# Layer 1 of a two-layer trunk: low weight parts from DRAM, an even/odd convolution on VectorE, and a 6:2 split of the channel tiles

## The chip, the cores and the metric

The kernel runs on one core of a Trainium2 chip. The metric is the device time of one execution in microseconds. A run's own time is a little longer than the span of its profile, which goes from the first to the last instruction. The engines are TensorE (PE; its weight loads PEld), VectorE (DVE), ScalarE (ACT), GpSimd (POOL) and SyncE (SP), which issues every DMA of this kernel, in program order.

## What is computed

A decoder trunk of two layers over 2048 positions of 1024 channels, each `x + RMSNorm_post(mixer(RMSNorm_pre(x)))`. Layer 0 is windowed attention beside a pooling mixer. Layer 1, which the change touches:

```python
def odd_mixer(h, w_in, dw_w, dw_b, ln_g, ln_b, w_out):
    proj = h @ w_in
    a, b, gate = jnp.split(proj, [CONV_WIDTH, 2 * CONV_WIDTH], axis=-1)
    glu = a * jax.nn.sigmoid(b)
    conv = lax.conv_general_dilated(
        glu, dw_w.astype(glu.dtype), window_strides=(1,), padding=[(CONV_K - 1, 0)],
        dimension_numbers=('NWC', 'WIO', 'NWC'), feature_group_count=CONV_WIDTH)
    cf = conv.astype(jnp.float32) + dw_b.astype(jnp.float32)
    mu = jnp.mean(cf, axis=-1, keepdims=True)
    var = jnp.mean(jnp.square(cf - mu), axis=-1, keepdims=True)
    cn = (cf - mu) * lax.rsqrt(var + EPS) * ln_g.astype(jnp.float32) + ln_b.astype(jnp.float32)
    y = jax.nn.silu(cn).astype(h.dtype) * jax.nn.silu(gate)
    return y @ w_out
```

## The kernel before

**Tiles and stages.** Channels lie on the 128 partitions, so 1024 channels are 8 tiles (k or i, 0 to 7). The 2048 positions are done in two halves of 1024, each in two blocks of 512 columns. Layer 0 runs for both halves, then layer 1: `inproj1` with `gates1` for half 0 and for half 1 (24 weight tiles of `wc` per half: for each channel tile the one of the tanh gate and the one of the value, then eight of the output gate), and then `outproj` with `wo1`, whose eight weight tiles are taken for each of four half and block pairs: 32 uses, called w0 to w31 here. w16 is the first of half 1, w24 the first of the last block.

**Products.** `project` makes a 512-column block of one weight tile with 24 matmuls: for each of 8 k, weights rounded to fp32r (`wh`) with the rounded part of the data (`hi`), `wh` with the rest of the data (`lo`), and the rest of the weights (`wl`) with `hi`. `w_load` brings raw weight tiles (512 KB) into three `wr` slots; `w_split` copies them to `wh` on ScalarE and forms `wl` as raw minus `wh` on VectorE. There are two slots each of `wh` and `wl`.

**Convolution.** For five of the eight channel tiles `conv_dve` runs 31 taps over 1024 columns per half on VectorE, two of them plain multiplies and 29 multiply-adds, in two alternating sums, and adds these. For three tiles (2, 4, 6) `conv_pe` does the taps of both halves as 16 groups of three 128x128 matmuls on TensorE with weights built on the host (`toep`). The results go through DRAM: `cd` (VectorE tiles), `ct` (TensorE tiles); the gates go through `sg`, a tile of two k for each half and block.

**Norm.** `norms` loads the eight results of a half, sums them, and for each block takes mean and variance (`norm_block`); `apply` then does for each k: times the reciprocal root, Silu, times the gate, and the split into `hi` and `lo`, the mix tile that `outproj` multiplies. Post-norm and residual of a finished block follow on VectorE while the next block is on TensorE.

**Order.** Nothing is written out by hand. `Flow` is a planner that runs while the program is built: the main line emits TensorE work, side tasks (generators with a priority) are stepped when their inputs are ready by the planner's own costs, and the order in which they emit is the order on each engine. `get` and `put` take and return slots of the SBUF pools (`s4` has 37 slots of 4 KB per partition), `until` waits for a condition. Each operation is recorded at one line, that of the helper (L189 before, L190 after), so the rows name tiles: `mm` products, `a` convolution or mean sums in PSUM, `s` a tile of the s4 pool, `packed` small constants.

Of the kernel before, what the change touches and what calls it, by code (L numbers as in the profile page):

```python
# [27 lines left out]
HIST = CK - 1  # L28
NJ = (CK + PH - 1 + PH - 1) // PH
# [5 lines left out]
DVE_CONV = (0, 1, 3, 5, 7)  # L35
# [9 lines left out]
    ("sinks", 8), ("post", 2 * KT), ("icnt", 64), ("tri", 2 * P), ("pscale", 4), ("dwn", len(DVE_CONV) * CK), ("dwb", KT), ("dwbp", KT * GPT),  # L45
# [162 lines left out]
def trunk_kernel(tc, a):  # L208
# [395 lines left out]
    gc = const([P, len(DVE_CONV), HIST], "gc")  # L604

    def constants():
# [7 lines left out]
        V.tensor_scalar(dwb, dwb, 2.0, None, op0=ALU.mult)  # L614
        V.tensor_scalar(dwbp, dwbp, 2.0, None, op0=ALU.mult)
# [410 lines left out]

    def conv_dve(half, i, slot, gl, over):
        acc = []
        for _ in range(2):
            acc.append((yield from get("s4")))  # L1030
        V.tensor_scalar(acc[0], gl[:, 0:TH], dwn[:, slot, 0:1], dwb[:, i:i + 1], op0=ALU.mult, op1=ALU.add)
        yield flow.t["P"]
        V.tensor_scalar(acc[1], gl[:, 1:1 + TH], dwn[:, slot, 1:2], None, op0=ALU.mult)
        for k in range(2, CK):
            yield flow.t["P"]
            r = acc[k % 2]
            V.scalar_tensor_tensor(r, gl[:, k:k + TH], dwn[:, slot, k:k + 1], r, op0=ALU.mult, op1=ALU.add)
# [54 lines left out]
    def glu(bank, at, ths, b, gv, n):  # L1092
# [42 lines left out]
    def apply(half, k, b, cfs, rbs, sgs, mix, done, left):  # L1135
# [4 lines left out]
        if key not in sgs:  # L1140
            yield from until(lambda: (half, *key) in stored)
# [4 lines left out]
        yield V.tensor_tensor(out=c, in0=c, in1=halves(g)[k % 2], op=ALU.mult)  # L1146
        t = yield from get("s4", TH, F32R)
# [10 lines left out]
    def norms(half, over, mix, done):  # L1158
        yield from until(lambda: len(over[half]) >= 5 and (half == 0 or len(dones[half - 1]) >= KT))
        cfs, rbs, sgs, left, loaded = {}, {}, {}, {}, []  # L1160

        def load():
            for n in range(KT):
                yield from until(lambda: len(over[half]) > n)
# [12 lines left out]
        for n in range(1, KT):  # L1177
# [168 lines left out]
```

## Time and profile before

| | before |
|---|---|
| median of 3 runs | 1501.53 us (1500.33 to 1501.77) |
| the profiled execution's own time | 1503.71 us |
| span of its profile | 1500.8 us |
| mean granted TensorE clock, share of full | 0.991 |
| TensorE busy | 1469.3 us (98%) |
| VectorE busy | 1250.2 us (83%) |
| ScalarE busy | 565.2 us (38%) |
| DMA | 186.46 MB, mean 124 GB/s |

In its profile, layer 1 begins at about 697 us, the out-projection of layer 1 at 1282 us, its half 1 at 1379 us, its last block at 1441 us. A line of --lines form reads: line, engine, operation, output<-inputs, shapes, count, then busy us and mean ns of one, then the engine's idle time just before and what ended it. Matmuls overlap in the records, so their mean exceeds their share of the time.

### The profile page before, as it was taken

How to read it: one execution, taken by the hardware profiler on the slowest of the kernel's cores; microseconds unless marked ns; L12 is line 12 of the kernel's file. 1: busy time of each engine (PE TensorE's matmuls, PEld its weight loads, DVE VectorE, ACT ScalarE, POOL GpSimd, SP SyncE). 2: the span in 40 equal slices, each digit the busy share in tenths (PEclk: the TensorE clock that was granted, in tenths of full speed). 3: DMA queues.
4: the chain of work that ended last, by engine and by line, in shares of the span. 5: the costliest groups of instructions: out<-in, count | busy, mean ns of one | idle time of the engine just before them, and what ended most of it. 6: DMA issues, size and time to landing. Idle time of an engine off the chain costs nothing.

```text
span 1500.8 us, 19112 instructions
## 1 busy us (share of the span) xinstructions
PE 1469.3 (98%) x7226; PEld 1193.0 (79%) x7226; DVE 1250.2 (83%) x1927; ACT 565.2 (38%) x1069; POOL 49.1 (3%) x65
## 2 busy tenths in 40 slices
PE   8999999999999999999999999999999999998997
PEld 6877778788877778788888888888888888776796
DVE  7888775777887766577899999999999999989885
ACT  6454432454444423454211123211212134666551
POOL 0000000000000000000100000000000000000000
PEclk9999999999999999999999999999999999999898
DMA  6112312455411101355421224422544744836574
GB/s 221 57 54 80 97 44 59 140 175 176 145 33 33 46 29 56 99 178 187 166 63 55 82 85 136 172 71 67 182 148 137 236 144 137 256 127 229 165 251 154
DMA packets 107468, 186.46 MB, mean 124 GB/s; under 512 B 32240, under 2 KB 56432, under 8 KB 107376
## 3 DMA queue, kind: packets, MB, share of 16 engines
q1 hardware_dynamic: 107376, 185.25, 39.3%
q8 instruction: 56, 0.92, 0.3%
q14 instruction: 36, 0.29, 0.1%
HBM read 146.42 MB, written 38.80 MB: 123 GB/s over the span
## 4 chain that ended last, share of the span: by engine, by line
PE 92%; DVE 3%; DMA 2%; ACT 1%; issue 1%; SPq 0%; POOL 0%; POOLq 0%; DVEq 0%; ACTq 0%
PE mm L189 81%; PE a L189 5%; PE pv L189 3%; PE pt L189 2%; DVE s L189 2%; DMA s<-in_toep 1%; DVE t L189 1%; DVE wl L189 0%; DMA s<-in_xn 0%; DMA gt<-s 0%; ACT s L189 0%; DMA s<-sg 0%; SPq L189 0%; ACT wh L189 0%; ACT t L189 0%
## 5 line engine op out<-in xcount | busy, mean ns | idle before, releaser
L189 PE MATMUL mm<-s,wh 128*128 128x512 f32 (+1 forms) x3616 | 1139.6, 396 | 13.3 <-ACT s L189 7.4
L189 PEld LDWEIGHTS mm<-s,wh 128*128 128x128 f32 x3616 | 669.5, 189 | 164.6 <-DVE s L189 10.7
L189 PE MATMUL mm<-s,wl 128*128 128x512 f32 (+1 forms) x1808 | 709.9, 393 | 0.0
L189 PEld LDWEIGHTS mm<-s,wl 128*128 128x128 f32 x1808 | 341.4, 189 | 76.2
L189 DVE SCALAR_TENSOR_TENSOR s<-s,packed,s 128x1024 f32<-128x1024 f32 x290 | 354.6, 1279 | 0.0
L189 ACT ACTIVATE wh<-wr 128x1024 fp32r<-128x1024 f32 (+1 forms) x138 | 145.4, 1054 | 368.8 <-PE mm L189 315.9
L189 DVE TENSOR_TENSOR wl<-wr,wh 128x1024 fp32r<-128x1024 f32 (+1 forms) x138 | 167.7, 1215 | 74.9 <-ACT wh L189 72.8
L189 ACT ACTIVATE t<-mm 128x512 f32<-128x512 f32 (+1 forms) x122 | 68.5, 562 | 98.6 <-PE mm L189 90.3
L189 DVE TENSOR_TENSOR t<-t,t 128x512 f32<-128x512 f32 (+1 forms) x131 | 86.2, 663 | 17.3 <-ACT t L189 15.4
L189 ACT ACTIVATE s<-mm 128x512 f32<-128x512 f32 (+1 forms) x116 | 67.9, 585 | 78.2 <-PE mm L189 70.8
L189 PE MATMUL a<-s,s 128*128 128x128 f32 (+2 forms) x592 | 90.5, 290 | 1.1 <-DMA s<-in_toep 0.9
L189 PEld LDWEIGHTS a<-s,s 128*128 128x128 f32 x592 | 81.1, 190 | 11.1 <-DMA s<-in_toep 2.8
L189 DVE TENSOR_TENSOR s<-s,s 128x512 f32<-128x512 f32 (+3 forms) x100 | 85.0, 874 | 3.3 <-DMA s<-ct 1.0
L189 ACT ACTIVATE s<-t 128x512 fp32r<-128x512 f32 (+1 forms) x52 | 48.8, 938 | 64.4 <-DVE t L189 64.1
L189 DVE TENSOR_TENSOR s<-t,s 128x512 fp32r<-128x512 f32 (+1 forms) x56 | 52.4, 935 | 22.1 <-ACT s L189 20.9
L189 ACT ACTIVATE t<-s 128x512 f32<-128x512 f32 x80 | 48.8, 628 | 50.7 <-DVE s L189 42.4
L189 DVE TENSOR_TENSOR t<-pt,packed 128x512 f32<-128x512 f32 x64 | 44.1, 690 | 28.4 <-PE pt L189 27.9
L189 ACT ACTIVATE s<-s,st 128x128 f32<-128x128 f32 x128 | 49.6, 389 | 25.0 <-DVE st L189 24.9
L189 POOL TENSOR_TENSOR rs<-ms,mhalf 128x4 f32<-128x4 f32 (+1 forms) x21 | 24.9, 1186 | 791.8 <-DVE ms L189 787.7
L189 DVE SCALAR_TENSOR_TENSOR s<-t,mm 128x512 f32<-128x512 f32 x48 | 40.1, 836 | 8.1 <-PE mm L189 6.2
L189 ACT ACTIVATE s<-xh 128x512 fp32r<-128x512 f32 x48 | 29.9, 630 | 39.9 <-DVE xh L189 39.5
L189 PEld LDWEIGHTS pv<-t,s 128*64 128x64 f32 x480 | 25.1, 136 | 23.2 <-issue 7.2
(100 smaller groups left out, 928.3 us busy)
## 6 DMA issues: line engine op xcount, KB each, us to landing
wr<-in_wo SPq DMA_DIRECT2D x64, 512.0 KB, 3.7
wr<-in_wc SPq DMA_DIRECT2D x48, 512.0 KB, 3.7
wr<-in_wa SPq DMA_DIRECT2D x27, 512.0 KB, 3.7
s<-in_toep SPq DMA_DIRECT2D x24, 384.0 KB, 4.3
xr<-in_xp SPq DMA_DIRECT2D x32, 256.0 KB, 4.1
x<-s SPq DMA_DIRECT2D x32, 256.0 KB, 3.2
xh<-x SPq DMA_DIRECT2D x32, 256.0 KB, 3.6
sg<-s SPq DMA_DIRECT2D x16, 512.0 KB, 4.8
```

What stands on the lines that cost most here:

```text
L189: fn(*args, **kw)
```

## The change

- `w_lows`, a task of low priority that starts at 60 us, forms the low parts of the 32 distinct layer 1 weight tiles once, during layer 0 (load, copy on ScalarE, subtract on VectorE, store to DRAM `wcl` and `wo1l`). `w_split` then loads `wl` by DMA in layer 1 and leaves out the subtract.
- `conv_dve` splits the positions by parity. `both` is even plus odd; three chains of half length run over even, odd and `both` (16, 15 and 16 taps, the last with sums of neighbouring taps), and even and odd outputs come from their sums and differences.
- Six channel tiles go to VectorE (0, 1, 3, 4, 6, 7), two to TensorE (2, 5).
- `norms` of half 1 starts when the program has emitted the last gate weight (`gated`), no longer when half 0's mix tiles are done; `apply` takes a gate load or a mix tile only if more than three s4 slots are free or `gated` holds; loads of results follow the additions (`added`); norm tasks of half 1 have a priority lower by one.

The diff, cut:

```diff
-DVE_CONV = (0, 1, 3, 5, 7)
+DVE_CONV = (0, 1, 3, 4, 6, 7)
...
+    def w_lows():
+        yield 60.0
+        for name, i in lows:
+            yield from until(lambda: avail["s4"] > 5)
+            raw = (yield from get("s4")).rearrange("p (k f) -> p k f", k=KT)
+            wl = (yield from get("s4", TH, F32R)).rearrange("p (k f) -> p k f", k=KT)
+            yield Q.dma_start(out=raw, in_=a[name][i])
+            yield A.activation(wl, raw, AF.Copy)
+            at = V.tensor_tensor(out=wl, in0=raw, in1=wl.bitcast(F32), op=ALU.subtract)
+            put(raw)
+            yield at
+            Q.dma_start(out=kept[name, i], in_=wl.bitcast(F32))
+            put(wl)
+            formed.add((name, i))
...
+                if (name, i) in kept:
+                    yield from until(lambda: (name, i) in formed)
+                    Q.dma_start(out=wl.bitcast(F32), in_=kept[name, i])
                 yield A.activation(wh[:, ks], raw[:, ks], AF.Copy)
-                V.tensor_tensor(out=wl[:, ks], in0=raw[:, ks], in1=wh[:, ks].bitcast(F32), op=ALU.subtract)
+                if (name, i) not in kept:
+                    V.tensor_tensor(out=wl[:, ks], in0=raw[:, ks], in1=wh[:, ks].bitcast(F32), op=ALU.subtract)
...
+        V.tensor_tensor(out=both, in0=even, in1=odd, op=ALU.add)
+        for m in range(HJ + 1):
+            for r, x, w, bias in ((ya, even, dwn[:, slot, HIST - 2 * m:CK - 2 * m], dwb), (yb, odd, dwn[:, slot, HIST - 1 - 2 * m:HIST - 2 * m] if m < HJ else None, None), (yc, both, dws[:, slot, HJ - m:HJ + 1 - m], dwb2)):
+                if w is None:
+                    continue
+                yield flow.t["P"]
+                xs = x[:, HJ - 1 - m:HJ + n - m] if x is odd else x[:, HJ - m:HJ + n - m]
+                if m:
+                    V.scalar_tensor_tensor(r, xs, w, r, op0=ALU.mult, op1=ALU.add)
...
+        V.tensor_tensor(out=cv[:, 0], in0=ya.rearrange("f (s q) -> f s q", s=SG), in1=yb[:, :n].rearrange("f (s q) -> f s q", s=SG), op=ALU.add)
+        V.tensor_tensor(out=ya, in0=ya, in1=yb[:, 1:], op=ALU.add)
+        yield flow.t["P"]
+        at = V.tensor_tensor(out=cv[:, 1], in0=yc.rearrange("f (s q) -> f s q", s=SG), in1=ya.rearrange("f (s q) -> f s q", s=SG), op=ALU.subtract)
...
         if key not in sgs:
-            yield from until(lambda: (half, *key) in stored)
+            yield from until(lambda: (half, *key) in stored and (avail["s4"] > 3 or gated))
             g = yield from get("s4")
             sgs[key] = (g, Q.dma_start(out=g, in_=sg_t[(half, *key)]))
...
+        yield from until(lambda: avail["s4"] > 3 or gated)
         t = yield from get("s4", TH, F32R)
...
-        yield from until(lambda: len(over[half]) >= 5 and (half == 0 or len(dones[half - 1]) >= KT))
+        yield from until(lambda: len(over[half]) >= 5 and (half == 0 or gated))
...
-                yield from until(lambda: len(over[half]) > n)
+                yield from until(lambda: len(over[half]) > n and added[0] >= n - 2)
...
-            flow.spawn(block(b), 1 + b)
+            flow.spawn(block(b), 1 + b + half)
...
         gates1(half, now)
+    gated.append(1)
```

**How the order moves, first place: SP where the out-projection begins.** `wr` is a raw weight tile, `wl` (from `wo1l`) a low part, `s<-sg` a gate tile, `s<-cd` and `s<-ct` results of the convolution, `sg<-s` a store; the waits in brackets are for lanes of the DMA queue or for engines. Before, from the raw tile of w3 on (the next one is that of w4):

```order
L189 DMA wr_10021<-in_wo 128x1024 [waits DMAHW6_49,DVE_49]
L189 DMA sg_3_0_102<-s_1549_9909 128x1024 [waits DMAHW7_49,Activation_49]
L189 DMA s_1576_10078<-sg_3_0_94 128x1024 [waits DMAHW0_49,PE_49]
L189 DMA s_1580_10107<-sg_0_1_89 128x1024 [waits DMAHW1_49,PE_49]
L189 DMA wr_10114<-in_wo 128x1024 [waits DMAHW2_49,DVE_49]
L189 DMA sg_3_1_103<-s_1559_9963 128x1024 [waits DMAHW3_49,Activation_49]
L189 DMA s_1585_10143<-cd_1_79 128x1024 [waits DMAHW4_49,PE_49]
L189 DMA s_1586_10145<-ct_75 128x16x64 [waits DMAHW5_49,PE_49]
L189 DMA s_1587_10147<-cd_1_81 128x1024 [waits DMAHW6_49,PE_49]
```

With the change, from the row behind the raw tile of w4 to the low part of w2:

```order
L190 DMA s_1633_10546<-sg_3_0_94 128x1024 [waits DMAHW6_49,DMAHW5_49,DVE_49]
L190 DMA s_1634_10548<-sg_3_0_94 128x1024 [waits DMAHW7_49]
L190 DMA s_1635_10550<-cd_1_77 128x1024
L190 DMA s_1636_10552<-ct_74 128x16x64 [waits DMAHW0_49]
L190 DMA s_1637_10554<-cd_1_79 128x1024 [waits DMAHW1_49]
L190 DMA s_1638_10556<-sg_0_1_89 128x1024 [waits DMAHW2_49]
L190 DMA s_1639_10558<-sg_0_1_89 128x1024 [waits DMAHW3_49]
L190 DMA s_1640_10560<-sg_1_1_91 128x1024 [waits DMAHW4_49]
L190 DMA sg_3_1_103<-s_1619_10414 128x1024 [waits DMAHW5_49,Activation_49]
L190 DMA s_1643_10602<-cd_1_81 128x1024 [waits DMAHW6_49]
L190 DMA s_1644_10604<-ct_75 128x16x64 [waits DMAHW7_49]
L190 DMA wl_10612<-wo1l_134 128x1024 [waits DMAHW0_49,PE_49]
```

Before, two gate tiles stood ahead of the raw tile of w4 and the loads of half 1 behind it, each with a wait for TensorE; now eleven transfers, most without such a wait, stand between the raw tile of w4 and the low part of w2, whose slot comes free with the last matmul of w0. Two gate tiles are loaded twice.

**Second place: SP where half 1 of the out-projection begins.** Before, the last two gate tiles of half 1's first block (2 and 3):

```order
L189 DMA wr_10918<-in_wo 128x1024 [waits DVE_49]
L189 DMA s_1735_10932<-sg_2_0_100 128x1024 [waits DMAHW4_49,PE_49]
L189 DMA out_y<-s_1624_10343 128x512 [waits DMAHW5_49,DVE_49]
L189 DMA out_y<-s_1624_10343 128x512 [waits DMAHW6_49,DVE_49]
L189 DMA xr_10938<-x_0_0_104 128x512 [waits DMAHW7_49,DMAHW1_49]
L189 DMA xr_10942<-x_0_0_104 128x512 [waits DMAHW2_49,DMAHW0_49]
L189 DMA s_1739_10949<-sg_3_0_102 128x1024 [waits PE_49]
```

With the change, the low part of w17 and a raw tile, then the same two gate tiles:

```order
L190 DMA wl_11403<-wo1l_133 128x1024 [waits DMAHW6_49,PE_49]
L190 DMA wr_11412<-in_wo 128x1024 [waits DMAHW7_49,Activation_49]
L190 DMA s_1803_11439<-sg_2_0_100 128x1024 [waits DMAHW0_49]
L190 DMA s_1808_11462<-sg_3_0_102 128x1024 [waits DMAHW1_49]
L190 DMA s_1809_11465<-sg_0_1_97 128x1024 [waits DMAHW2_49]
```

The gate tiles now come behind a low part that waits for the last matmul of w15.

**Third place: DVE, up to the last mix tile of w16's block.** Before, from the multiply by the last gate tile to the subtract that forms the last `lo`:

```order
L189 TENSOR_TENSOR s_1591_10155<-s_1591_10155,s_1739_10949 128x512 [waits DMAHW1_49]
L189 TENSOR_TENSOR s_1627_10363<-s_1627_10363,t_1702_10746 128x512
L189 TENSOR_SCALAR ms_10986<-pt_10978 128x4 [waits PE_49]
L189 CAST rh_10991<-rs_10989 128x4 [waits Pool_49]
L189 TENSOR_TENSOR s_1749_10993<-s_1591_10155,s_1749_10993 128x512 [waits Activation_49]
L189 TENSOR_TENSOR s_1627_10363<-s_1627_10363,s_1739_10949 128x512 [waits Activation_49]
L189 TENSOR_TENSOR rh_10991<-rs_10989,rh_10991 128x4 [waits DVE_49]
L189 CAST rh_11004<-rs_10999 128x4 [waits Pool_49]
L189 TENSOR_TENSOR s_1753_11008<-identr,rh_10991 128x512
L189 TENSOR_TENSOR s_1753_11008<-identr,rh_10991 128x512 [waits DVE_49]
L189 TENSOR_TENSOR rh_11004<-rs_10999,rh_11004 128x4 [waits DVE_49]
L189 TENSOR_TENSOR s_1752_11006<-s_1627_10363,s_1752_11006 128x512 [waits Activation_49]
```

With the change, the last twelve rows of such a piece, which begins 14 rows higher with the multiply that waits for gate tile 2; `x2` is a row for two instructions, 28 in all, one of them on four columns:

```order
L190 TENSOR_TENSOR s_1816_11497<-s_1659_10672,s_1816_11497 128x512 [waits Activation_49]
L190 TENSOR_TENSOR s_1691_10878<-s_1691_10878,t_1775_11297 128x512
L190 TENSOR_TENSOR s_1817_11504<-s_1635_10550,s_1817_11504 128x512 [waits Activation_49]
L190 TENSOR_TENSOR s_1637_10554<-s_1637_10554,s_1809_11465 128x512
L190 TENSOR_TENSOR s_1636_10552<-s_1636_10552,t_1792_11391 128x512
L190 TENSOR_TENSOR s_1738_11114<-s_1738_11114,xr_11491 128x512 [waits DMAHW7_49,DVE_49]
L190 TENSOR_TENSOR s_1691_10878<-s_1691_10878,s_1808_11462 128x512 [waits Activation_49]
L190 TENSOR_TENSOR s_1738_11114<-s_1738_11114,xr_11494 128x512 [waits DMAHW0_49,DVE_49]
L190 TENSOR_TENSOR s_1818_11514<-s_1637_10554,s_1818_11514 128x512 [waits Activation_49]
L190 TENSOR_TENSOR s_1643_10602<-s_1643_10602,t_1792_11391 128x512
L190 SCALAR_TENSOR_TENSOR s_1761_11231<-s_1761_11231,packed,t_1811_11475 128x512 x2
L190 TENSOR_TENSOR s_1819_11517<-s_1691_10878,s_1819_11517 128x512 [waits Activation_49]
```

Before, from the first multiply with gate tile 2 to that last subtract there were 21 instructions, six of them on tiles of four columns (`ms`, `rh`); now post-norm and residual of half 0's second block (`packed`, `xr`) stand among them.

## Rows read from the trace of the kernel before

**Rows 1.** The page, busy time and 40 slices.
```profile
PE 1469.3 (98%) x7226; PEld 1193.0 (79%) x7226; DVE 1250.2 (83%) x1927; ACT 565.2 (38%) x1069; POOL 49.1 (3%) x65
...
PE   8999999999999999999999999999999999998997
...
DVE  7888775777887766577899999999999999989885
```

**Rows 2.** Windows: us; PE, PEld, DVE, ACT, POOL busy; granted clock, DMA share, GB/s.
```profile
697.00:1282.00 585.00, 583.97 (x2695) 480.56 (x2694) 547.57 (x547) 141.53 (x230) 22.23 (x26) 1.00 0.41 128
60.00:543.00 483.00, 479.43 (x2610) 378.33 (x2609) 372.26 (x897) 211.35 (x511) 13.42 (x16) 1.00 0.29 88
1282.00:1441.00 159.00, 150.17 (x633) 119.48 (x632) 142.81 (x211) 92.98 (x142) 5.16 (x4) 0.95 0.62 199
1050.00:1100.00 50.00, 49.20 (x261) 41.20 (x260) 46.76 (x43) 9.31 (x22) 1.06 (x4) 1.00 0.50 154
1385.00:1390.00 5.00, 3.06 (x10) 2.41 (x11) 4.04 (x9) 2.00 (x4) 1.44 (x1) 0.55 0.83 319
1440.00:1450.00 10.00, 10.00 (x87) 10.00 (x86) 8.40 (x14) 6.83 (x12) 1.01 (x1) 1.00 1.00 327
```

**Rows 3.** The chain that ended last: start us, us, step; three like these two.
```profile
1060.22 2.94 PE a L189 x24
...
1174.08 2.68 PE a L189 x24
```

**Rows 4.** Groups of instructions by form, whole span.
```profile
L189 DVE SCALAR_TENSOR_TENSOR s<-s,packed,s 128x1024 f32<-128x1024 f32 x290 | 354.6, 1279 | 0.0
L189 DVE SCALAR_TENSOR_TENSOR s<-s,packed,t 128x512 f32<-128x512 f32 x56 | 40.1, 746 | 4.0 <-ACT t L189 4.0
L189 ACT ACTIVATE wh<-wr 128x1024 fp32r<-128x1024 f32 (+1 forms) x138 | 145.4, 1054 | 368.8 <-PE mm L189 315.9
L189 DVE TENSOR_TENSOR wl<-wr,wh 128x1024 fp32r<-128x1024 f32 (+1 forms) x138 | 167.7, 1215 | 74.9 <-ACT wh L189 72.8
```

**Rows 5.** ScalarE in order of time: start us, us, copies of w1, w2, w3.
```profile
1282.33 1.06 ACT L189 ACTIVATE wh<-wr 128x1024 fp32r<-128x1024 f32 x1 [0.64 <-PE mm L189]
...
1289.01 1.06 ACT L189 ACTIVATE wh<-wr 128x1024 fp32r<-128x1024 f32 x1 [0.57 <-ACT s L189]
...
1294.56 1.06 ACT L189 ACTIVATE wh<-wr 128x1024 fp32r<-128x1024 f32 x1 [1.78 <-PE mm L189]
```

**Rows 6.** SP in order of time: start us, us, issue.
```profile
1284.68 0.33 SPq L189 DMA_DIRECT2D wr<-in_wo  x1
...
1296.20 3.85 SPq L189 DMA_DIRECT2D s<-sg  x1
...
1380.66 0.38 SPq L189 DMA_DIRECT2D s<-sg  x1
```

**Rows 7.** DMA issues, us to landing: whole span twice, then at 1284.68, 1296.20, 1380.66, 1400:1450.
```profile
wr<-in_wo SPq DMA_DIRECT2D x64, 512.0 KB, 3.7
s<-sg SPq DMA_DIRECT2D x16, 512.0 KB, 5.4
wr<-in_wo SPq DMA_DIRECT2D x1, 512.0 KB, 4.3
s<-sg SPq DMA_DIRECT2D x1, 512.0 KB, 7.7
s<-sg SPq DMA_DIRECT2D x1, 512.0 KB, 5.3
s<-x SPq DMA_DIRECT2D x2, 512.0 KB, 7.2
```

**Rows 8.** TensorE in order of time: the start of w16, its last k.
```profile
1379.48 0.49 PE L189 MATMUL mm<-s,wh 128*128 128x512 f32 x1
...
1397.27 0.80 PE L189 MATMUL mm<-s,wh 128*128 128x512 f32 x1 [0.88 <-DVE s L189]
```

**Rows 9.** VectorE in order of time, from the multiply with gate tile 2.
```profile
1386.07 1.29 DVE L189 TENSOR_TENSOR s<-s,s 128x512 f32<-128x512 f32 x2 [0.93 <-DMA s<-sg]
...
1396.53 0.68 DVE L189 TENSOR_TENSOR s<-s,s 128x512 fp32r<-128x512 f32 x1
```

More of the change, by code (lines that the diff above doesn't have):

```diff
@@ L322, in trunk_kernel @@
     wraw, wready, last = [], [], set()
+    lows = [x for n, x in enumerate(wseq) if x[0] in ("wc", "wo1") and x not in wseq[:n]]
+    kept = {(name, i): dr.tile([P, KT, P], F32, tag=f"{name}l_{i}", name=f"{name}l_{i}") for name, i in lows}
+    formed = set()
+    def w_lows():
[12 more added lines that the diff above has]
+            formed.add((name, i))
     def w_load(go):
@@ L614, in constants @@
         V.tensor_scalar(dwb, dwb, 2.0, None, op0=ALU.mult)
+        V.tensor_scalar(dwb2, dwb, 2.0, None, op0=ALU.mult)
+        pairs_of = dwn[:, :, 1:].rearrange("p i (m r) -> p i m r", r=2)
+        V.tensor_tensor(out=dws[:, :, 1:], in0=pairs_of[:, :, :, 0], in1=pairs_of[:, :, :, 1], op=ALU.add)
+        V.tensor_copy(dws[:, :, :1], dwn[:, :, :1])
         V.tensor_scalar(dwbp, dwbp, 2.0, None, op0=ALU.mult)
@@ L1025, in last_block, with parities @@
             put(*w)
+    def parities(gl):
+        return gl.rearrange("f (r j) -> f r j", r=2)
     def conv_dve(half, i, slot, gl, over):
[L1028 to L1037, printed above, removed]
+        n = TH // 2
+        even, odd = parities(gl)[:, 0, :], parities(gl)[:, 1, :]
+        ta = yield from get("s4", 2 * n + HJ)
+        tb = yield from get("s4", 2 * n + 1)
+        both, ya = ta[:, :n + HJ], ta[:, n + HJ:]
+        yb, yc = tb[:, :n + 1], tb[:, n + 1:]
+        V.tensor_tensor(out=both, in0=even, in1=odd, op=ALU.add)
[7 more added lines that the diff above has]
+                    V.scalar_tensor_tensor(r, xs, w, r, op0=ALU.mult, op1=ALU.add)
+                elif bias is None:
+                    V.tensor_scalar(r, xs, w, None, op0=ALU.mult)
+                else:
+                    V.tensor_scalar(r, xs, w, bias[:, i:i + 1], op0=ALU.mult, op1=ALU.add)
@@ L1095, in glu @@
         th = ths[b]
-        at = V.scalar_tensor_tensor(
-            gv[:, b * PB:(b + 1) * PB, :], th.rearrange("f (p s) -> f p s", p=PB), 1.0,
-            bank.rearrange("f (p s) -> f p s", p=PB), op0=ALU.add, op1=ALU.mult)
+        if gv is None:
+            at = V.scalar_tensor_tensor(gl[:, cols(b)], th, 1.0, bank, op0=ALU.add, op1=ALU.mult)
+        else:
+            for r in range(2):
+                tr, br = (t.rearrange("f (q r s) -> f q r s", r=2, s=SG)[:, :, r] for t in (th, bank))
+                at = V.scalar_tensor_tensor(gv[:, b * PB // 2:(b + 1) * PB // 2, r], tr, 1.0, br, op0=ALU.add, op1=ALU.mult)
         put(th, bank)
@@ L1186, in block @@
             yield from norm_block(b, cfs, rbs)
-            yield from spread_tasks([apply(half, k, b, cfs, rbs, sgs, mix, done, left) for k in range(KT)], 3, 1 + b)
+            yield from spread_tasks([apply(half, k, b, cfs, rbs, sgs, mix, done, left) for k in range(KT)], 3, 1 + b + half)
             put(rbs[b])
         for b in range(NB):
-            flow.spawn(block(b), 1 + b)
+            flow.spawn(block(b), 1 + b + half)
         yield from until(lambda: len(rbs) == NB)
         put(total)
-    stored = set()
+    stored, gated = set(), []
     def gate_out(half, j, b, sg, ready):
```

29 lines of the change are left out of this document (17 added, 12 removed).

## The prediction

> **What bounds the kernel now.** I read the page's busy times and slices first. TensorE is busy 98% of the span [rows 1], so a change gains by taking work from it or by closing one of its few gaps, and loses by opening new ones. The windows, read second, show where the gaps are. From 697 to 1282 us, the in-projection of layer 1 with the convolution, TensorE is busy 583.97 of 585 us and VectorE 547.57; in layer 0, from 60 to 543 us, TensorE 479.43 of 483 and VectorE 372.26; from 1282 to 1441 us, the first three blocks of the out-projection, TensorE is idle for 9 of 159 us and the granted clock falls to 0.95, with VectorE at 142.81 [rows 2]. VectorE's high share in the first of these stretches costs nothing by itself; only in the last one does TensorE wait for it. The chain of waits names the convolution's matmuls as path work of TensorE [rows 3]. Last, I read the order in time around the two places where the change moves loads: the start of the out-projection [rows 5, 6] and the start of its half 1 [rows 8, 9].
>
> I make the sum against the profiled execution's own time, 1503.71 us, which is 2.2 above the median of the runs, 1501.53; the forecast is then lowered by 2.2. About 0.2%, 3 us, is what a measurement of this kernel can tell from no change.
>
> **The change part by part.**
>
> *One convolution tile leaves TensorE.* The rows show groups of 24 records, 12 matmuls, in 2.68 us; a tile of 16 groups of three matmuls has four of them: 4 x 2.68 = 10.7 us off the path. The loads of its weights go too: of the 0.8 us that TensorE was idle between 1050 and 1100 us [rows 2], and the first group's 2.94 against 2.68 [rows 3], I take **-1**. Together **-11.7**.
>
> *VectorE in the in-projection.* The 1024-column multiply-add takes 354.6/290 = 1.22 us, the 512-column one 40.1/56 = 0.72 [rows 4]. A tile and half cost about 29 x 1.22 + 3 = 38.4 us and will cost 47 x 0.72 + 3 = 36.8; ten of these before are 384, twelve after 442. The 48 subtracts of `wl` here go, 48 x 1.22 = 58. So VectorE stays at 547.6 + 58 - 58 = 548 us beside a TensorE of 574, covered as before: **0**.
>
> *The low parts in layer 0.* 32 copies of 1.05 us are 34 us on ScalarE, 32 subtracts of 1.22 are 39 on VectorE [rows 4], with 32 loads and 32 stores on a DMA that is 0.29 busy there. They have low priority, and VectorE has 111 us free in 483 [rows 2]. Bounds 0 (all hidden) and 4 (the idle time that TensorE already has there, once more); nearest are the present gaps, where side tasks hide well: **+1**.
>
> *The start of the out-projection.* Call T0 the last matmul of the gate weights. The copies of w1, w2 and w3 each wait for the end of the weight two before, and stand at 1282.33, 1289.01 and 1294.56 [rows 5]: so T0 is about 1282.3, a weight takes 5.55 us, and w2 starts at T0 + 12.2, with 1.1 of stall. In the new order the low part of w2 comes behind eleven half-megabyte transfers, which come behind the raw tile of w4, which waits for the copy of w1, so they begin at T0 + 1.9 (the copy takes 1.05 and starts 0.6 after its weight; an issue follows). The nearest burst is in the trace: ten half-megabytes issued from 1284.68 to 1296.20 [rows 6], the first landing after 4.3 us at 1289.0, the last after 7.7 at 1303.9 [rows 7]: nine in 14.9, 1.66 each. At a DMA share of 1.00 it moved 327 GB/s [rows 2], 1.6 us for half a megabyte. A load alone lands after 3.7 [rows 7]. Twelve transfers from T0 + 1.9 end at 1.9 + 3.7 + 11 x 1.6 = T0 + 23.2. w1 is done earlier (the last gate tile, now issued at T0 + 1.9, lands by T0 + 7.3 at the median of 5.4 [rows 7], and its k ends w0 by about T0 + 14). So w2 starts at T0 + 23 instead of T0 + 12.2: **+10.8**, between 8 (transfers that overlap better, 1.35 each) and 13 (1.8 each).
>
> By the Trainium skill, "DMA: Bandwidth & Descriptors", section "Queues, rings and completion order", each DMA engine takes the descriptors of a ring in order, so a late row pays for those ahead of it; if it did not, this term would be 0 and the sum 1500. The landings that grow from 4.3 to 7.7 us in the burst agree, though no row shows a ring by itself.
>
> *Later in half 0* one store and reload of a result stands ahead of the low part of w8: **+0.7** (0 to 1.4), half of one transfer of 1.6 that the lead of one weight doesn't take.
>
> *The start of half 1.* Call T1 the start of w16, 1379.48; its last k was ready at 1397.27, T1 + 17.8 [rows 8], and the clock sank to 0.55 meanwhile [rows 2]. The gate tile of row 1380.66 [rows 6] landed 5.3 us later [rows 7], and from there, 1386.07, VectorE needed 11.1 us [rows 9] for 21 instructions, six of them on four columns. Now that gate tile comes behind the low part of w17, which waits for w15's end, and behind a raw tile: issue at T1 + 1.9, landing at T1 + 7.2. Then 27 instructions of 0.645 us (1.29 for two [rows 9]) are 17.4: T1 + 24.6, **+6.8**. VectorE no longer has the subtract of `wl` and so reaches this piece sooner, though it waits there for the gate tile; I take **+6**, between 0 (as before) and 9 (the second gate tile late by one transfer).
>
> *The last block.* The low part of w25 comes behind two loads of x, which landed after 7.2 us [rows 7]; its lead is one weight, 5.55, less 1 for what precedes its issue: 7.2 - 4.6 = **+2.6** (0 to 4).
>
> *The other low parts* land after 3.7 us (the raw tile of the same size [rows 7]), under the 5.55 of a weight: **0**, up to 6 where raw tiles stand ahead of them.
>
> Sum: -11.7 + 1 + 10.8 + 0.7 + 6 + 2.6 = +9.4; 1503.7 + 9.4 - 2.2 = **1511**. All low bounds give -3.7 (1498), all high ones +25.7 (1527).
>
> **The rivals.**
>
> 1. *Faster: the loads are hidden and VectorE's relief closes the gap at w16.* In the stretch from 1282 to 1441 VectorE was 142.81 of 159 us busy [rows 2], and some 24 subtracts of 1.22, 29 us, go. If the low part of w2 lands by the end of w1 (T0 + 12.2, so 0.6 us per transfer), and post-norm is done early enough for the last mix tile at about T1 + 8, the sum is -11.7 + 1 - 10 = -20.7: 1481. It decides by whether those eleven transfers take more or less than 8 us. If half of each comes true, -11.7 + 1 + 5 - 5 = 1491. For it: the relief is real. Against it: 327 GB/s at a full DMA, and a gate tile that is issued after w15's end whatever VectorE does.
>
> 2. *No change: the stall at T0 only just eats the convolution tile.* T0 costs 8, half 1 and the last block together 2.5: -11.7 + 1 + 8 + 2.5 = -0.2: 1501. For it: each of these is within its bounds.
>
> 3. *The low parts bound the out-projection.* With two slots a load starts when the weight two before ends; if landing takes L > 5.55, a weight takes (L + 5.55)/2. Under a full DMA loads took 7.2 [rows 7]: 0.8 more for 20 weights, 16 us: 1527. Against it: DMA is 0.62 busy there [rows 2] and a raw tile's median is 3.7.
>
> 4. *VectorE becomes the bound of the in-projection.* What it has there without convolution and subtracts is 547.6 - 384 - 58 = 106 us; 574 leaves 39 per tile and half, so it decides at 36/47 = 0.77 us per multiply-add. The mean of one was 0.746 [rows 4], near, but overlapped. At 0.80, 12 x 47 x 0.03 = 17 us late: 1528. The Trainium skill speaks against shorter operations, "VectorE: DVE Perf Modes", section "The TRN2 errata": a fixed cost per instruction, 691 ns for 512 columns by its formula, 1224 for 1024. The trace agrees at 1.22 and has 0.72 for the short one; by the page's figure VectorE would have 16 us more room, and this rival would be rarer still.
>
> **How the numbers follow.** My forecast, with the bursts over the conv tile's worth: 0.48. Rival 1, both forms: 0.24, of which 0.09 lies below 1489. Rival 2: 0.15. Rival 3: 0.08. Rival 4: 0.05. So faster 0.24, same 0.15, slower 0.48 + 0.08 + 0.05 = 0.61. The range goes from 1489 (most of rival 1's milder form) to 1525: it leaves out about 0.09 below and 0.1 above, the upper parts of rivals 3 and 4. The likeliest case's own range is 1505 to 1525.
>
> **What would show it.** Right: after the end of the gate weights TensorE idles about 11 us before w2, released by a DMA of `wl`; the `wl` load there lands some 20 us behind the first of the burst; w16's last k comes about 24 us after w16's start; from 697 us to T0 the time is some 11 us shorter; convolution multiply-adds of 0.66 to 0.75 us. Wrong: w2 starting within 14 us of T0, w16's last k earlier than 17 us, or `wl` waits spread evenly over all weights.

## The result, and the profile after

| | before | changed |
|---|---|---|
| median | 1501.65 us (4 runs) | 1518.66 us (4 runs, 1516.12 to 1519.03) |
| ratio to before | | 1.011, 95% interval 1.0093 to 1.0128 |
| own time of the profiled execution | 1503.71 us | 1518.69 us |
| span of the profile | 1500.8 us | 1516.9 us |

The change makes the kernel 17 us slower; 1511 was forecast, with a range of 1489 to 1525. In what follows a copy is ScalarE's `wh<-wr`, and T0, as in the prediction, the end of the gate weights. First the page and the windows of the changed kernel (us; PE, PEld, DVE, ACT, POOL busy; granted clock, DMA share, GB/s), which answer to [rows 1, 2]:

```profile
PE 1465.0 (97%) x7130; PEld 1184.3 (78%) x7130; DVE 1222.0 (81%) x2198; ACT 588.5 (39%) x1085; POOL 62.3 (4%) x66
```

```profile
697.00:1282.00 585.00, 576.45 (x2598) 470.80 (x2596) 519.97 (x806) 142.88 (x221) 35.91 (x27) 1.00 0.52 171
60.00:543.00 483.00, 481.30 (x2597) 382.27 (x2597) 389.44 (x906) 228.01 (x531) 12.02 (x16) 1.00 0.39 128
1282.00:1441.00 159.00, 138.15 (x556) 106.34 (x557) 122.40 (x198) 84.14 (x131) 4.65 (x4) 0.89 0.79 269
```

TensorE is busy 4 us less in all, and VectorE 28; the loss is in the third row, where TensorE is idle for 21 us in place of 9 and the clock falls to 0.89. To place it, ScalarE in order of time (start us, us, in brackets the idle time before and what ended it), the copies of w1 to w4, as in [rows 5]:

```profile
1274.28 1.06 ACT L190 ACTIVATE wh<-wr 128x1024 fp32r<-128x1024 f32 x1 [0.85 <-PE mm L190]
1289.84 1.06 ACT L190 ACTIVATE wh<-wr 128x1024 fp32r<-128x1024 f32 x1 [3.88 <-PE mm L190]
1296.47 1.06 ACT L190 ACTIVATE wh<-wr 128x1024 fp32r<-128x1024 f32 x1 [2.49 <-PE mm L190]
1305.27 1.06 ACT L190 ACTIVATE wh<-wr 128x1024 fp32r<-128x1024 f32 x1 [0.28 <-ACT s L190]
```

T0 is 1274.3, 8.0 us earlier than before. Then w0 takes 15.5 us, w1 6.6 and w2 8.8, where a weight takes 5.55. TensorE, SP (issues) and DMA (us to landing: the gate tile of 1275.81, the result of 1287.85, the low part of 1290.21) in the same stretch:

```profile
1284.09 0.79 PE L190 MATMUL mm<-s,wh 128*128 128x512 f32 x1 [5.47 <-ACT s L190]
...
1300.04 0.50 PE L190 MATMUL mm<-s,wl 128*128 128x512 f32 x1 [2.97 <-DMA wl<-wo1l]
```

```profile
1274.46 0.32 SPq L190 DMA_DIRECT2D wl<-wo1l  x1
...
1275.81 0.84 SPq L190 DMA_DIRECT2D s<-sg  x2
...
1287.85 0.53 SPq L190 DMA_DIRECT2D s<-ct  x1
1290.21 5.91 SPq L190 DMA_DIRECT2D wl<-wo1l  x1
```

```profile
s<-sg SPq DMA_DIRECT2D x1, 512.0 KB, 6.8
...
s<-ct SPq DMA_DIRECT2D x1, 512.0 KB, 10.9
...
wl<-wo1l SPq DMA_DIRECT2D x1, 512.0 KB, 9.8
```

The gate tile, issued at T0 + 1.5 and landed at T0 + 8.4, stalls w0. The low part of w2 is issued at T0 + 15.9: SP was through the burst at 1288.4 and then waited 1.7 us for the end of w0 (1289.84), which frees the slot. It lands at T0 + 25.7 (1300.0), 1.3 us behind the load ahead of it (1287.85 + 10.9 = 1298.7). So the transfers ahead of it set its landing, and the wait for w0 was covered by them.

At the start of half 1, VectorE in order of time; the row of 1392.93 is the first multiply with gate tile 2, that of 1409.28 the last `lo`. Below it SP's issue of gate tile 2 (the first of the three) and its time to landing:

```profile
1391.66 1.28 DVE L190 TENSOR_TENSOR s<-s,t 128x512 f32<-128x512 f32 x2
1392.87 0.16 DVE L190 CAST rh<-rs 128x4 fp32r<-128x4 f32 x1
1392.93 0.68 DVE L190 TENSOR_TENSOR s<-s,s 128x512 f32<-128x512 f32 x1
...
1397.22 0.74 DVE L190 SCALAR_TENSOR_TENSOR s<-s,packed,t 128x512 f32<-128x512 f32 x1
...
1409.28 0.68 DVE L190 TENSOR_TENSOR s<-s,s 128x512 fp32r<-128x512 f32 x1
```

```profile
1386.77 1.37 SPq L190 DMA_DIRECT2D s<-sg  x3
```

```profile
s<-sg SPq DMA_DIRECT2D x1, 512.0 KB, 5.7
```

From 1387.98 to the last `lo` no row has idle time before it: VectorE did not wait for the gate tile, it was busy until it came to it. But the tile had landed at 1392.5, only 0.4 us earlier, so two limits end at the same time here. In no run was VectorE idle for a gate tile for more than 1.7 us in all while w16 was on TensorE (r3).

Earlier VectorE had room. From w2's end to w15's end, in the changed kernel and then before (columns as in the windows above):

```profile
1305.30:1385.30 80.00, 78.60 (x348) 63.10 (x347) 63.44 (x105) 43.97 (x69) 3.33 (x3) 1.00 0.76 258
```

```profile
1300.10:1377.40 77.30, 76.72 (x338) 61.75 (x337) 70.03 (x103) 46.35 (x73) 2.33 (x2) 1.00 0.53 174
```

It was idle for 16.6 us against 7.3, most of it waiting for tiles of ScalarE (6.8), loads of x (4.3) and a result (3.0). So the amount of its work alone does not make it late at w16; when its inputs come counts as well, and no run separates the two.

The whole way, at the copies that wait for the end of the weight two before, in us; "last" is the span less w25's copy:

| | first copy of layer 1 | T0 (w1) | w2's end (w4) | w15's end (w17) | w16's end (w18) | w25's copy | last |
|---|---|---|---|---|---|---|---|
| before | 702.7 | 1282.3 | 1300.1 | 1377.4 | 1398.2 | 1439.9 | 60.9 |
| changed | 698.1 | 1274.3 | 1305.3 | 1385.3 | 1410.8 | 1451.8 | 65.1 |

From column to column the changed kernel gains 4.6, gains 3.4, loses 13.2, 2.7 and 4.7, gains 0.7 and loses 4.2: 16.1, the difference of the spans.

Not every one of these is clear of noise. Run r5 below has the same instructions as the changed kernel in the same order up to about 1335 us, yet its T0 is 1271.7, 2.5 us sooner; run r10 and the kernel before are alike in the same way, and its first copy of layer 1 stands at 701.4 and its T0 at 1281.2, 1.3 and 1.1 sooner. So a difference of 1 to 3 us in one place between two profiles tells nothing by itself.

### The profile page after: what moved, and what is told of

It reads as the page before. It is cut to its first block, busy times and chain, and to the rows that moved or that the text cites. A ratio compares the mean times of both kernels' runs of the same rounds, so it can differ in the third digit from the quotient of the medians.

```text
span 1516.9 us, 19421 instructions
## 1 busy us (share of the span) xinstructions
PE 1465.0 (97%) x7130; PEld 1184.3 (78%) x7130; DVE 1222.0 (81%) x2198; ACT 588.5 (39%) x1085; POOL 62.3 (4%) x66
## 5 line engine op out<-in xcount | busy, mean ns | idle before, releaser
L190 PE MATMUL mm<-s,wh 128*128 128x512 f32 (+1 forms) x3616 | 1141.5, 396 | 25.5 <-ACT s L190 15.5
L190 DVE SCALAR_TENSOR_TENSOR s<-s,packed,s 128x512 f32<-128x512 f32 (+1 forms) x348 | 248.3, 748 | 0.0
L190 DVE TENSOR_TENSOR s<-s,s 128x512 f32<-128x512 f32 (+4 forms) x158 | 138.8, 891 | 21.7 <-ACT s L190 6.4
L190 DVE SCALAR_TENSOR_TENSOR s<-s,dws,s 128x512 f32<-128x512 f32 x180 | 134.4, 748 | 0.0
L190 DVE TENSOR_TENSOR wl<-wr,wh 128x1024 fp32r<-128x1024 f32 (+1 forms) x64 | 77.2, 1207 | 40.1 <-ACT wh L190 38.6
L190 PE MATMUL a<-s,s 128*128 128x128 f32 (+2 forms) x496 | 80.3, 298 | 4.5 <-DMA s<-in_toep 4.4
L190 PEld LDWEIGHTS a<-s,s 128*128 128x128 f32 x496 | 71.0, 194 | 13.8 <-issue 4.1
L190 DVE SCALAR_TENSOR_TENSOR s<-t,mm 128x256 f32<-128x256 f32 (+1 forms) x72 | 44.4, 676 | 37.8 <-PE mm L190 30.1
L190 ACT ACTIVATE s<-s 128x1024 fp32r<-128x1024 f32 (+1 forms) x64 | 53.2, 843 | 44.5 <-DMA s<-in_wc 19.2
L190 ACT ACTIVATE s<-t 128x512 fp32r<-128x512 f32 (+1 forms) x52 | 48.7, 940 | 50.5 <-DVE t L190 50.1
```

The costliest lines, as they stand in the source:

```text
L190: fn(*args, **kw)
```

## The experiments

Three theories. **Queue**: low parts wait behind bursts on SP's queue, and that sets the end. **Gate tile**: the end is set by the gate tiles that are issued late. **VectorE**: the end is set by what VectorE has to do by the last mix tile of w16's block. The runs, at the same copies (medians in us, ratios to before with their 95% intervals; in r4 the copies of w1 and w4, and in r6 that of w4, stood behind other waits, told below):

| run | T0 | w2's end | w15's end | w16's end | median | ratio |
|---|---|---|---|---|---|---|
| r1, wo1's low parts by subtract | 1270.4 | 1299.1 | 1374.3 | 1416.0 | 1518.61 | 1.0122 (1.0107 to 1.0137) |
| r2, old gating | 1273.7 | 1303.8 | 1382.4 | 1406.1 | 1512.42 | 1.0077 (1.0060 to 1.0094) |
| r3, low parts one weight ahead | 1276.3 | 1305.6 | 1384.2 | 1411.4 | 1514.43 | 1.0095 (1.0080 to 1.0110) |
| r4, r2 and r3 together | 1299.8 | 1321.4 | 1405.0 | 1411.1 | 1515.63 | 1.0102 (1.0087 to 1.0117) |
| r5, post-norm late | 1271.7 | 1303.3 | 1381.4 | 1396.3 | 1506.09 | 1.0037 (1.0024 to 1.0051) |
| r6, r2 and another queue | 1273.6 | 1302.8 | 1384.4 | 1408.0 | 1515.36 | 1.0097 (1.0079 to 1.0115) |
| r7, r1 and r2 together | 1269.9 | 1286.5 | 1361.7 | 1413.8 | 1517.57 | 1.0111 (1.0096 to 1.0126) |
| r8, Toeplitz loads ahead | 1269.7 | 1304.4 | 1381.0 | 1412.5 | 1518.89 | 1.0118 (1.0101 to 1.0135) |
| r9, r5 and r7 together | 1270.3 | 1286.9 | 1362.1 | 1412.2 | 1516.23 | 1.0097 (1.0081 to 1.0112) |
| r10, before with post-norm late | 1281.2 | 1299.0 | 1377.3 | 1396.0 | 1498.65 | 0.9984 (0.9975 to 0.9994) |
| r11, r1, r5 and r8, gate tiles once | 1269.9 | 1298.0 | 1372.9 | 1423.1 | 1525.35 | 1.0157 (1.0140 to 1.0174) |
| r12, five tiles to three | 1284.0 | 1308.7 | 1393.8 | 1400.2 | 1510.52 | 1.0079 (1.0061 to 1.0098) |

The change itself is at 1.0093 to 1.0128. Of the edits to it, r5 alone is clearly faster than that; the intervals of r2 and r12 just reach it.

**r1. The out-projection's low parts by VectorE again.**

```diff
-    lows = [x for n, x in enumerate(wseq) if x[0] in ("wc", "wo1") and x not in wseq[:n]]
+    lows = [x for n, x in enumerate(wseq) if x[0] == "wc" and x not in wseq[:n]]
```

> Low parts kept for the in-projection's weights alone; those of the out-projection formed by the VectorE subtract again, all else as changed (1518.7 us). Theory Q (queue): the stall at T0 has two causes that overlap, the last gate tile issued after T0 (w0 done at T0 + 15.5) and the low part of w2 behind the burst (w2 starts at T0 + 25.7). Without the second, w2 starts at about T0 + 21, 5 us sooner, and the 4 us at the last block go; the gap at half 1 stays. About 1509 to 1513. Theory V (VectorE): what is lost in the out-projection is norm work on VectorE that comes in one burst; 32 more subtracts of 1.2 us there make it worse: 1520 to 1535.

Neither time came: 1518.6, as with the whole change. In place Queue was right in part: w15 ends 11 us sooner (3.9 by T0, 2.3 from there to w2's end, where 5 were expected, and 4.8 behind it), and the last block costs nothing more. VectorE was right too: w16 then takes 41.7 us, against 25.5 with the change and 20.8 before. What one place gained the other took back.

**r2. The old gating.**

```diff
-            yield from until(lambda: (half, *key) in stored and (avail["s4"] > 3 or gated))
+            yield from until(lambda: (half, *key) in stored)
...
-        yield from until(lambda: len(over[half]) >= 5 and (half == 0 or gated))
+        yield from until(lambda: len(over[half]) >= 5 and (half == 0 or len(dones[half - 1]) >= KT))
...
-            flow.spawn(block(b), 1 + b + half)
+            flow.spawn(block(b), 1 + b)
```

(and, the same way, the other free-slot wait, the pacing by `added` and the priority of `apply`.)

> The conditions of norms and apply as they were before the change (start of half 1's norms, free slots, pacing of loads, priorities), all else as changed. The last gate tile of w0's block is then issued about 10 us ahead of T0. Theory Q: w0 no longer stalls, but the low part of w2 is still behind nine transfers and starts at about T0 + 20 instead of T0 + 25.7: about 1512 to 1514. Theory G (late gate tile alone): the whole stall at T0 goes, 13 us: about 1505.

1512.4, the number that Queue had. w0 and w1 take 5.5 and 5.9 us and w2 waits alone, TensorE in order of time:

```profile
1296.91 0.79 PE L190 MATMUL mm<-s,wl 128*128 128x512 f32 x1 [11.59 <-DMA wl<-wo1l]
```

But T0 to w2's end is 30.1 us against 31.0, hardly less; of the 4.7 us that the profile is ahead at w16's end, 1.5 came by w2's end. So Queue's number came, but not at the place that it named: that is luck. Gate tile alone is out, since the stall at T0 stayed.

**r3. Low parts one weight ahead.**

```diff
+    def w_kept():
+        yield from until(lambda: begun)
+        for name, i in [x for x in wseq if x in kept][:-(KT - 2)]:
+            yield from until(lambda: (name, i) in formed)
+            wl = yield from get("wl", dt=F32R)
+            Q.dma_start(out=wl.bitcast(F32), in_=kept[name, i])
+            kl.append(wl)
...
```

(three `wl` slots, 36 slots in place of 37 in s4.)

> Three slots for low parts instead of two (one slot less of the s4 pool) and their loads issued by a task of their own, one weight earlier, so that the low part of w2 stands ahead of the burst; gating as changed. Theory Q: w2 starts when w0, late by its gate tile, and w1 are done, T0 + 21: about 5 us less at T0 and the 4 us at the last block: 1509 to 1514. Theory G: nothing at T0, at most the last block's 4: 1515 or more. If neither holds and each weight is slowed by the DMA traffic itself: 1518.

1514.4, between the two ranges. No weight waits for its low part at T0 any more, yet T0 to w2's end is 29.3, with w0 at 16.3 by its gate tile. So either cause alone (r2, r3) costs about as much as both: they overlap, as Queue said, and r7, where neither is left, has 16.6 there. w16 ends at 1411.4, where it ended with the change; the gain came at the last block, which takes 61.1 us from w25's copy in place of 65.1.

**r4. r2 and r3 together.**

> Both of the former: low parts one weight ahead and the old gating. Theory Q: neither cause is left, w2 starts within 14 us of T0: about 13 us less at T0 and up to 4 at the last block, 1502 to 1506 (it falls below 1502 only if half 1 gains too). Theory G: as with the old gating alone, 1505. Were the causes independent and additive, the two single gains would add up; under Q the sum of the singles is smaller than the gain of both at T0.

No theory's number: 1515.6. TensorE stood still for a weight copy, and ScalarE, which makes it, waited for VectorE with the copy behind that wait, in the planner's order; VectorE did convolution from 1275 to 1292 (ScalarE in order of time):

```profile
1296.66 0.81 ACT L190 ACTIVATE s<-s,packed 128x512 f32<-128x512 f32 x1 [24.92 <-DVE s L190]
1297.38 1.04 ACT L190 ACTIVATE wh<-wr 128x1024 fp32r<-128x1024 f32 x1
```

```profile
1298.47 1.22 PE L190 MATMUL mm<-s,wh 128*128 128x512 f32 x2 [19.46 <-ACT wh L190]
```

(the second fence is TensorE.) This new wait hides what the two edits give together at T0. VectorE's convolution ended at 1292.0 here, 29 us sooner than with the change; w15 ended 20 us later, and w16 then took 6.0 us without a wait. That it ended at 1411.1, the time of the changed kernel, shows nothing: TensorE's own 19.5 us set it here, not VectorE.

**r5. Post-norm late.**

```diff
-            flow.spawn(finish(), 1)
+            flow.spawn(finish(), 4 if layer else 1)
```

> As changed (1518.7 us), but in the out-projection the post-norm and residual of a finished block get a priority lower than the norm work of half 1, so that fewer of their instructions stand on VectorE ahead of the last mix tile of w16's block. Theory V (at the start of half 1 TensorE waits for VectorE's work in its order, not for the gate tiles): the gap there, some 22 us of which 5 are new, shrinks by 4 to 8 us: 1511 to 1515. Theory L (the late gate tiles set it): no change at that place, 1518 within 2.

1506.1, 12.6 us less than the change: more than VectorE forecast. w16 takes 14.9 us in place of 25.5. The edit is to post-norm's priority alone, but the planner then also issued gate tiles 2 and 3 earlier, ahead of w15's end (1381.4); SP in order of time:

```profile
1375.57 1.27 SPq L190 DMA_DIRECT2D s<-sg  x2
```

So post-norm ahead of the mix tiles on VectorE and the late issue of the gate tiles went together, and this run doesn't tell what each of them gave. Some of it returns at the last block, which takes 68.8 us from w25's copy in place of 65.1.

**r6. The low parts of wo1 on GpSimd's queue, with the old gating.**

```diff
+    W = Engine(flow, "S", nc.gpsimd)
...
-                    Q.dma_start(out=wl.bitcast(F32), in_=kept[name, i])
+                    (W if name == "wo1" else Q).dma_start(out=wl.bitcast(F32), in_=kept[name, i])
```

> The old gating (1512.4 us), and the low parts of the out-projection loaded by GpSimd's queue in place of SP's, so that neither the issue nor the lanes stand behind the burst. With the old gating alone w2 waited 11.6 us for its low part at T0. Theory Q: that wait falls to 0 to 4 us, the end comes 8 to 12 us sooner: 1500 to 1504. If the delay were the DMA engines' own (all of them full of the burst), w2 would wait as before: 1512. If GpSimd's waits hold up the roots of the post-norm behind them, 2 to 5 us are lost again at half 1.

1515.4, missed. TensorE, VectorE and ScalarE have the same order of work as in r2. The wait of 11.59 fell to 1.06, but w4 waited for its copy, which on ScalarE stood behind a wait for VectorE. TensorE, then ScalarE:

```profile
1286.30 0.50 PE L190 MATMUL mm<-s,wl 128*128 128x512 f32 x1 [1.06 <-DMA wl<-wo1l]
...
1303.94 1.22 PE L190 MATMUL mm<-s,wh 128*128 128x512 f32 x2 [6.79 <-ACT wh L190]
```

```profile
1302.31 0.63 ACT L190 ACTIVATE s<-s 128x512 fp32r<-128x512 f32 x1 [14.25 <-DVE s L190]
1302.85 1.04 ACT L190 ACTIVATE wh<-wr 128x1024 fp32r<-128x1024 f32 x1
```

So SP's queue held the low part, that is shown; that it set the end is not, since VectorE and ScalarE were as late. What the run then loses at the last block (62.9 us from w25's copy) and between is more than with the old gating alone, and was not looked into.

**r7. r1 and r2 together.**

> Low parts kept for the in-projection alone (as in the first run, 1518.6 us) and the old gating. In the first run T0 cost 8 us less than with the whole change but half 1 lost 20 against before. Theory V with the gating at fault (half 1's norms of lower priority and started early): T0 costs nothing and half 1 is as before, so that what was gained by T0 (11 us) is left: 1490 to 1496. Rival: the 32 subtracts in the out-projection are what VectorE can't do beside the six tiles' norms: half 1 loses 15 to 20 as before: 1508 to 1516.

The rival's number nearly, 1517.6, and the clearest run. T0 costs nothing: w15 ends at 1361.7, 16 us ahead of before and 24 ahead of the change. Then w16 takes 52 us and ends at 1413.8, 3 us behind the change. Windows as above, and TensorE in order of time:

```profile
1360.00:1380.00 20.00, 6.13 (x28) 4.58 (x26) 19.93 (x38) 9.30 (x16) 2.33 (x2) 0.66 0.39 139
1380.00:1400.00 20.00, 9.37 (x22) 5.86 (x22) 19.06 (x32) 7.44 (x11) 1.44 (x1) 0.50 0.66 227
```

```profile
1379.98 1.30 PE L190 MATMUL pv<-s,onesr 128*128 128x512 f32 x2 [4.69 <-DVE s L190]
...
1388.83 1.84 PE L190 MATMUL pt<-ones,t 128*128 128x1 f32 x8 [7.55 <-DVE t L190]
```

VectorE is busy for 39 of 40 us and TensorE for 15.5, at a clock down to 0.50: the small matmuls of statistics stand ahead of w16 and wait for VectorE.

**r8. Three Toeplitz loads in flight.**

```diff
-                while len(tts) < 2 and nt[0] < GPT // 2:
+                while len(tts) < 3 and nt[0] < GPT // 2:
```

> As changed (1518.7 us), but three of the TensorE convolution's weight loads in flight instead of two. In the changed kernel TensorE waits 4.4 us for these loads (0.9 us in all before), since each low and raw weight stands ahead of one on SP. If these waits are on the path: 3 to 4 us less at T0, and in the end as much, 1514 to 1516, unless the later stalls take it back (they are set by the burst and VectorE): 1518.

T0 came 4.6 us sooner than in the changed kernel, but only 2.1 sooner than in r5, which is the same up to there. TensorE's waits for these loads, 1040 to 1215 us (total, times, longest), in the changed kernel, in r5 and here:

```profile
PE a L190 <- DMA s<-in_toep: 4.4, 4, 2.5
```

```profile
PE a L190 <- DMA s<-in_toep: 3.9, 3, 1.7
```

```profile
PE a L190 <- DMA s<-in_toep: 2.7, 3, 1.2
```

They fell by 1.2 to 1.7 us; that they are on the path to T0 fits, more is not shown.

The end did not move: 1518.9, as the second expectation had it, with w16's end at 1412.5.

**r9. r5 and r7 together.**

> Low parts for the in-projection alone, the old gating, and late post-norm: the run that was 15 us ahead of the kernel before at the end of half 0's out-projection and lost 30 at half 1 (1517.6), with the edit that took 12 us off that place elsewhere. Theory V: the order on VectorE is the cause, and 12 or more of the 30 come back: 1502 to 1506, less what post-norm then costs at the last block (up to 9, as in the fifth run). If VectorE's amount of work sets it rather than its order: 1514 or more.

1516.2, as the second expectation had it: not the order of post-norm. w16 still takes 50.1 us, of which VectorE is idle for 2.0. The late post-norm helped with the change (r5), and not here, where the 32 subtracts are on VectorE again.

**r10. The kernel before with post-norm late.**

> The kernel before with the late post-norm alone. It too has a gap at the start of half 1, 18 us from w16's start to its last k. Theory V: there as well post-norm stands ahead of the mix tiles, so 5 to 12 us come back there, and 0 to 9 are lost at the last block: 1491 to 1500. If the gap before was set by the gate tiles (a load that landed late released VectorE there): no change, 1501.

1498.65, within what VectorE had, at its small end: 2.4 us faster than before. In place it is a miss: w16 takes 18.8 us for 20.8, 2 us less where 5 to 12 were expected. It is the only version that beats both kernels, by little.

**r11. r1, r5 and r8 with each gate tile loaded once.**

```diff
             yield from until(lambda: (half, *key) in stored and (avail["s4"] > 3 or gated))
-            g = yield from get("s4")
-            sgs[key] = (g, Q.dma_start(out=g, in_=sg_t[(half, *key)]))
+            if key not in sgs:
+                g = yield from get("s4")
+                sgs[key] = (g, Q.dma_start(out=g, in_=sg_t[(half, *key)]))
```

> Low parts for the in-projection alone, the changed gating with each gate tile loaded once, three convolution weight loads in flight, late post-norm. By the first run and the eighth it reaches T0 11 us ahead of before and loses some 8 there. Theory V: half 1 costs 12 less than the 20 of the first run: 1503 to 1508. If the in-projection's gain is always taken back by VectorE at half 1: 1512 or more.

1525.4, the slowest, although T0 came 4.4 us ahead of the change: w16 ended at 1423.1. Gains ahead of T0 go nowhere with six tiles and the subtracts on VectorE. The four edits are not told apart here.

**r12. Five tiles to three.**

```diff
-DVE_CONV = (0, 1, 3, 4, 6, 7)
+DVE_CONV = (0, 1, 3, 5, 7)
```

> As changed (1518.7 us), but with five tiles on VectorE and three on TensorE as before (0, 1, 3, 5, 7 and 2, 4, 6). The third tile costs TensorE 10.7 us, of which the changed kernel showed 4.6 gained against before at T0, so T0 comes 5 to 11 us later. On VectorE the last multiply-add of the convolution stood at 1293 us before and at 1321 with six tiles. Theory V: with five it ends at 1290 to 1300, the norms of half 1 begin sooner and half 1 costs 8 to 12 us less; the stall at T0 (a late gate tile and the queue) stays: 1513 to 1521. Theory T (the tile on TensorE is the only thing that the split changes): 1524 to 1530.

1510.5, below the ranges of both theories: giving the tile back to TensorE makes the changed kernel 8 us faster by the medians (its four runs go from 1508.5 to 1515.1). T0 comes 9.7 us later, and w16 takes 6.4 us in place of 25.5. Windows of this run, then VectorE's last multiply-add of the convolution here, in the changed kernel and before:

```profile
697.00:1282.00 585.00, 580.43 (x2670) 475.37 (x2669) 464.58 (x719) 146.91 (x235) 13.29 (x26) 1.00 0.55 179
1380.00:1400.00 20.00, 17.81 (x75) 14.29 (x75) 15.41 (x26) 13.72 (x22) 0.86 (x1) 0.91 0.83 314
```

```profile
1269.55 0.74 DVE L190 SCALAR_TENSOR_TENSOR s<-s,dws,s 128x512 f32<-128x512 f32 x1
```

```profile
1320.70 0.75 DVE L190 SCALAR_TENSOR_TENSOR s<-s,dws,s 128x512 f32<-128x512 f32 x1
```

```profile
1291.84 2.48 DVE L189 SCALAR_TENSOR_TENSOR s<-s,packed,s 128x1024 f32<-128x1024 f32 x2
```

With five tiles VectorE is done with the convolution 51 us sooner than with six and the gate tile no longer stalls w0. What is left are waits for low parts: 6.5 us in w2, which takes 13.6, 4.4 from there to w15's end, and 3.7 behind w16, where the last block takes 65.7 from w25's copy. The short w16 gives most of this back.

## Why the prediction was right, and where it was not

The direction and the range held; 17 us where 9.4 were forecast. In part that is luck: layer 0 came out shorter by about as much as was lost in the in-projection. Against the spans, by its own steps:

- *One convolution tile, -11.7.* r12 against the change gives 9.7 at T0, against r5 12.3: right within noise. But against before T0 gains only 8.0 (6.9 against r10). Layer 0 came out 4.6 us shorter (first copy of layer 1 at 698.1; 3.3 against r10), where +1 was forecast; the planner set another order there and which part of it gains was not tried. In layer 1 some 6 us are lost ahead of T0: r12 has as much TensorE work as before, begins layer 1 at 698.5, 4.2 ahead of before, and reaches T0 1.7 behind it. The low parts of the in-projection, whose loads the forecast put at 0 with a bound of 6, are the likely cause, but no run leaves them out. Waits for Toeplitz loads are part of it: 4.4 us in the changed kernel and 0.9 before; where the rest goes is open.
- *The start of the out-projection, +10.8 and +0.7.* Measured 13.2 and 2.7. The queue was named rightly: the low part of w2 came behind eleven transfers and landed at T0 + 25.7 for a forecast of 23.2. The transfers took 1.58 us each, as forecast (from the gate tile's landing at 1282.7 to 1300.0, eleven in 17.3); what was short is the first landing, T0 + 8.4 for 5.6, since the 3.7 us taken for a load alone is the median of all raw tiles and the gate tile took 6.8. What the prediction had for w0, an end at T0 + 14, came at 15.5. It is a second cause in the same place: with the low part out of the queue (r3) w2's end is still only 1.7 us nearer to T0. So its sign, 11 us of TensorE waiting for `wl` before w2, failed: that wait was 2.97. The Trainium skill's "DMA: Bandwidth & Descriptors" (section "Queues, rings and completion order") has descriptors taken in the order of the ring. The landings in order of issue agree, the low part's 1.3 us behind that of the row ahead of it. Part of the delay comes ahead of the ring, in SP: in r2 the low part was issued at 1290.7, 11.5 us behind the end of w0 that freed its slot; on another queue (r6) its wait went from 11.59 to 1.06.
- *The last block, +2.6.* Measured 4.2; r1, r7 and r9, where its low parts are not loaded, and r3, where they are loaded earlier, lose nothing there.
- *The start of half 1, +6.* Measured 4.7. The forecast of this place came out closely: gate tile 2 landed 7.2 us behind w15's end and the last `lo` ended 24.6 behind it, both as the prediction had them. But "though it waits there for the gate tile" was wrong: VectorE had no idle time to wait in. That its own earlier work ended within 0.4 us of the landing is luck. r5 took 10.7 us off this place.
- *"VectorE stays at 547.6 + 58 - 58 = 548 us beside a TensorE of 574, covered as before: 0".* This is the step that failed. The sum of the stretch was even less, 519.97, but it does not tell when VectorE is done. With six tiles its convolution ends 28 us later than before, with 25 multiply-adds behind T0, and norms of half 1 come behind it. In the changed kernel, r3 and r8 (six tiles, no subtracts, post-norm early) w16 ended at 1410.8 to 1412.5, and with the old gating (r2, r6) at 1406.1 and 1408.0, though T0 to w2's end ranged from 29 to 35 us. With the subtracts (r1, r7, r9, r11) it ended at 1412 to 1423, though w15 ended at 1362 to 1374, up to 24 us sooner than with the change. There the terms don't add up along TensorE: the stalls at T0 and the path through VectorE run side by side, and the later one counts. r7 removed the whole T0 term, put 32 subtracts back, and gained 1 us.
- *Rival 4* (VectorE as the bound of the in-projection) named the engine but looked for it by the busy share of that stretch; TensorE waited for VectorE not there but at the start of half 1.

So the sixth tile brings T0 9.7 us sooner and w16's end 10.6 us later (r12), and the low parts, which relieve VectorE, cost time at bursts: in r12, 10 us over before by the medians, TensorE waits 14.6 us for them. Each of three edits (post-norm late, five tiles, old gating) gives part of the loss back; all three together were not tried.

## What to carry to other kernels

Moving work to an engine that is idle on average is not free if that engine must be done at a certain point: compare the time at which it ends its backlog with the time at which its product is first needed, before and after, not its busy share. Where several stalls lie in a row on the busiest engine, ask for each whether another engine runs on through it; if so, taking the first one away only makes the next one longer. A load that replaces arithmetic needs a lead longer than the longest burst ahead of it on its queue.

## What the hardware showed that was not expected

A multiply-add over 512 columns takes 0.75 us by its record, but in a chain of three sums the next one starts 0.66 us later (1268.22, 1268.89, 1269.55 in r12). An estimate from that is 31 us for 47 taps, where the prediction put in 34 (47 x 0.72, from the busy time of post-norm's multiply-adds). The forecast for VectorE's busy time in the stretch was too high by 28 us, in part by this and in part because some of the convolution ran behind the stretch; its end was still too late.
